# Vectors of the last layer made for one condition, and spread three and six over two feed-forwards

## The chip, the cores and the metric

The kernel runs on one core of a Trainium2 chip. The metric is the device time of one execution in microseconds (us). Before the change it is 2590.86 us, the median of three runs (2588.58 to 2592.14).

## The reference, cut to what matters

The model has two layers over 512 latent tokens and 256 context tokens of width 1024. Each layer has a feed-forward half-step, a mixer and another feed-forward half-step. Nine vectors of 1024 numbers (shift, scale and gate for each of the three parts) steer a layer; they come from a matrix product with w_mod, once for the latents' condition c and once for the context's condition c_ctx:

```python
mx = jnp.split((silu(c) @ w_mod[l] + b_mod[l])[:, None, :], 9, axis=-1)
my = jnp.split((silu(c_ctx) @ w_mod[l] + b_mod[l])[None, None, :], 9, axis=-1)
x = x + 0.5 * mx[2] * swiglu(modulate(rmsnorm(x), mx[0], mx[1]), ...)
y = y + 0.5 * my[2] * swiglu(modulate(rmsnorm(y), my[0], my[1]), ...)
ox, oy = mixer(modulate(rmsnorm(x), mx[3], mx[4]), modulate(rmsnorm(y), my[3], my[4]), ...)
x = x + mx[5] * ox
if not last: y = y + my[5] * oy
x = x + 0.5 * mx[8] * swiglu(modulate(rmsnorm(x), mx[6], mx[7]), ...)
if not last: y = y + 0.5 * my[8] * swiglu(modulate(rmsnorm(y), my[6], my[7]), ...)
```

In the last layer my[5] to my[8] are read by nothing. The output is the RMS norm of the latents.

## The kernel before, in words

Activations lie transposed, with the model's width on the partitions: eight tiles of 128 rows for each stream. Products are made in three passes from a high and a low part (`mm3`, lines 162 to 167). Weights arrive as 512 KB tiles, are cast on ScalarE (line 159) and their rest is subtracted on VectorE (line 160), three tiles ahead of their use. At most four high and four low parts are held at a time.

*The vectors.* `mod_chunks` (line 364) makes them on VectorE. One vector, numbered j from 0 to 8, has two halves of 512 columns, and each half is four chunks of 512 KB. A chunk holds two row blocks; each of them is multiplied by the condition and added into an accumulator, one per condition (`mod_add`: line 319 for the first, line 321 for the others). So a chunk is four VectorE operations of 128x512. After four chunks `mod_fold` turns and reduces each accumulator (lines 329 and 330), and after two halves `mod_sums` adds up over partitions with one small matmul on TensorE (line 337) and adds the bias on VectorE (line 346). The chunk loads (line 371, on SyncE's queue) go into two buffers, `wm`; the load of a chunk waits until the chunk two before it has been added.

*The order of the work.* All instructions are issued in one order that a planner sets. `spent` counts a planner's clock by the columns of the products, and after each group of products `poll` lets every background task whose time has come issue its next step. `spawn(..., 90.0)` starts a task 90 planner us later. In `mod_chunks` a `yield -pace` makes the next step due one pace after the last due time, and `yield 11.71` sets it 11.71 after the present clock. `drain(task)` (line 124) issues everything that is left of a task at once, other tasks that are due before it included, and moves the planner's clock up to it. Each engine then works through its own queue in the order of issue.

*The stages around the change.* The second feed-forward of layer 0 and the first of layer 1 are both `ffn_halved` (line 808), over both streams, 22 blocks of 128 columns. The first four blocks are made directly; the other 18 by `up_halved`, seven products instead of eight, whose sums are copied (line 774) and added (lines 788 to 803). At the end of each, the down products of the context and then of the latents update x and its squares, and `done` starts `norm_steps` (line 487) as a task: mean square, reciprocal root, a broadcast through TensorE (line 450), and eight tiles of the normed input (lines 511 to 517). In the last layer the mixer begins with `keys` (line 961): the four key heads for the context, then for the latents.

Before the change, layer 1's vectors 0 to 4 are made during layer 0's second feed-forward, and 5 to 8 during layer 1's first. Both tasks are drained when their feed-forward has been issued:

```python
later = self.spawn(self.mod_chunks([(l, j) for j in range(5, 9)], 9.0), 90.0)      # 1395
self.ffn_halved(l, 0, h, both, both, both, done)
self.drain(later)                                                                # 1397
```

Of the kernel before, what the change touches and what calls it, by code (L numbers as in the profile page):

```python
# [20 lines left out]
DEPTH = 2  # L21
# [8 lines left out]
CTX, LAT = 0, 1  # L30
# [51 lines left out]
class Kernel:  # L82
# [229 lines left out]
        yield  # L312
        self.mod_sums(l, j, (half,), rows[:, :32])

    def mod_add(self, acc, raw, k):
        for v in range(2):
            s = self.sc[:, k, v : v + 1]
            if k == 0:
                self.nc.vector.tensor_scalar(acc[v], raw, s, None, op0=ALU.mult)
            else:  # L320
                self.nc.vector.scalar_tensor_tensor(acc[v], raw, s, acc[v], op0=ALU.mult, op1=ALU.add)  # L321

    def mod_fold(self, acc, rows):

        nc = self.nc
        rv = rows.rearrange("p (v b) -> p v b", v=2)
        for v in range(2):
            t = self.slot("mturn")
            nc.vector.transpose(t, acc[v])
            nc.vector.tensor_reduce(rv[:, v], t.rearrange("p (b i) -> p b i", i=32), axis=mybir.AxisListType.X, op=ALU.add)  # L330
# [33 lines left out]
    def mod_chunks(self, ljs, pace):  # L364

        nc = self.nc
        steps = [(l, j, half, kk) for l, j in ljs for half in range(2) for kk in range(4)]

        def load():
            raw = self.wide("wm").rearrange("p (k n) -> p k n", k=2)  # L370
            nc.sync.dma_start(raw, self.ins["w_mod"][steps.pop(0)])
            return raw

        after = load()
        for l, j in ljs:
            rows = self.tiny(64, "mrow")
            for half in range(2):
                acc = [self.slot("macc") for _ in range(2)]
                for kk in range(4):
                    raw, after = after, load() if steps else None  # L380
                    yield -pace
                    for k in range(2):
                        self.mod_add(acc, raw[:, k], kk * 2 + k)
                self.mod_fold(acc, rows[:, half * 32 : half * 32 + 32])
            yield 11.71
            self.mod_sums(l, j, (0, 1), rows)

# [927 lines left out]
    def run(self):  # L1315
        nc = self.nc
        both = (G_CTX, G_LAT)
        halves = (G_LAT1, G_LAT2)
        self.setup()
        raws = [self.mod_load(0, 1, 0)]  # L1320
        self.load_x(CTX, self.ins["ct"])
        self.load_x(LAT, self.ins["xt"])
        raws.append(self.mod_load(0, 0, 0))
        accs, bc = {}, {}
        h = self.rows()
        for grp in both:
            for dt in range(KD):
                self.square(dt, grp, accs)
        scale = self.mod_direct(0, 1, 0, raws[0])
        for _ in range(KD + 1):  # L1330
            next(scale)
        shift = self.mod_direct(0, 0, 0, raws[1])
        ms = [self.mean_square(G_CTX, accs)]
        for _ in range(2):
            next(shift)
        ms.append(self.mean_square(G_LAT, accs))
        r = self.rsqrt(ms, NT // P, 1.0 / D, "rms")
        dg = {G_CTX: self.diag(r[:, : NTT[CTX]]), G_LAT: self.diag(r[:, NTT[CTX] :])}
        next(scale, None)
        self.scale(0, 0, LAT, 0)  # L1340
        for _ in range(KD - 1):
            next(shift)
        for grp in both:
            ps = self.rstd(grp, dg[grp])
            bc[grp] = self.slot("rstd")[:, : grp[2]]
            nc.scalar.copy(bc[grp], ps)
        next(shift, None)
        with self.tc.issue_after(self.last.ins):
            w0 = {0: self.w13()}
        raws = [self.mod_load(0, 1 - j, 1) for j in range(2)]  # L1350
        for grp in both:
            self.norm_tiles(0, 0, grp, h, range(4), bc[grp])
        self.look = LOOKAHEAD
        with self.tc.issue_after(self.last.ins):
            w0[1] = self.w13()
        scale = self.mod_halfway(0, 1, 1, raws[0])
        next(scale)
        ps = {}
        begin = ((G_CTX, 0), (G_LAT, 0), (G_LAT, 1))
        for grp, f in begin:  # L1360
            ps[grp, f] = {(f, m): self.psum("up")[:, : grp[2]] for m in range(2)}
            self.products([(ps[grp, f][f, m], w0[f][m], 0) for m in range(2)], h, grp, range(4), last=False)
        shift = self.mod_direct(0, 0, 1, raws[1])
        for _ in range(KD + 1):
            next(shift)

        def begun(g):
            next(scale, None)
            next(shift, None)
            for grp in both:  # L1370
                self.norm_tiles(0, 0, grp, h, range(4, KD), bc[grp])
            for grp, f in begin:
                self.products([(ps[grp, f][f, m], w0[f][m], 512) for m in range(2)], h, grp, range(4, KD), first=False)
                self.up({f: w0[f]}, [f], h, g, grp, ps[grp, f])
            self.up(w0, [1], h, g, G_CTX)

        self.early = True
        self.first = [self.spawn(self.mod_chunks([(0, 2)], 4.0), 10.0)]
        later = self.spawn(self.mod_chunks([(0, j) for j in range(3, 9)], 6.0), 80.0)
        for l in range(DEPTH):  # L1380
            last = l == DEPTH - 1
            grps = (G_LAT,) if last else both
            cuts = halves if last else both

            def next_norm(l, idx):
                tiles = self.rows()
                return tiles, lambda grp, accs: self.norm(l, idx, grp, accs, tiles)

            h1, done = next_norm(l, 1)
            if not last:  # L1390
                self.ffn(l, 0, h, both, both, both, done, begun)
                self.drain(later)
                self.decays()
            else:
                later = self.spawn(self.mod_chunks([(l, j) for j in range(5, 9)], 9.0), 90.0)
                self.ffn_halved(l, 0, h, both, both, both, done)
                self.drain(later)

            h2, done = next_norm(l, 2)
            self.mixer(l, h1, grps, cuts, done)  # L1400

            if not last:
                later = self.spawn(self.mod_chunks([(l + 1, j) for j in range(5)], 7.4), 90.0)
                h, done = next_norm(l + 1, 0)
            else:
                done = self.final
            (self.ffn if last else self.ffn_halved)(l, 1, h2, cuts, grps, cuts, done)
            self.drain(later)
        self.drain(*self.tasks)
# [133 lines left out]
```

## Time and profile before

| what | us |
|---|---|
| median of three runs | 2590.86 |
| the profiled execution's own time | 2592.09 |
| its span, first to last instruction | 2590.3 |
| VectorE busy | 1811.2 (70%) |
| ScalarE busy | 1015.7 (39%) |

The profile is of one execution, on the one core, with a mean granted TensorE clock of 0.99. Busy time of TensorE is modelled: matmuls overlap in its pipeline, and idle time between them is more telling than the share. A wait is put down to the instruction whose end released it.

### The profile page before, as it was taken

To read this page: it belongs to the slowest core of one execution; us is meant where nothing else is said; L and a number is where in the kernel's file an instruction comes from. 1 tells how busy PE (TensorE), PEld (TensorE's weight loads), DVE (VectorE), ACT (ScalarE), POOL (GpSimd) and SP (SyncE) were. 2 spreads that over 40 slices of the span, in tenths; PEclk is the share of its full clock that TensorE was granted. 3 is DMA by queue.
4 is the path that set the end of the run, shared out by engine and by line. 5 is a ranking of instruction groups with operands and counts; after the bars stand their busy time and mean duration, and the time that the engine had idled before them with its cause. 6 is when DMAs were issued, how large, how long until landed. Compare 5 with 4: busy or idle time off the path is not lost. (4 is left out here: it accounts for less than half of the span.)

```text
span 2590.3 us, 36708 instructions
## 1 busy us (share of the span) xinstructions
PE 2529.6 (98%) x14002; PEld 2246.6 (87%) x14002; DVE 1811.2 (70%) x3390; ACT 1015.7 (39%) x1780; POOL 276.6 (11%) x316
## 2 busy tenths in 40 slices
PE   8999999999999999999999999999999999999998
PEld 4888888888888888999899889989998888888887
DVE  6957767747977677788788858758777786633345
ACT  3211211223335444555454445545544263422223
POOL 0000000000000122422320132322310001000000
PEclk9999999999999999999999999999999999999999
DMA  7533433422222745787775457776663334232231
GB/s 273 161 108 122 139 122 114 130 74 100 85 79 60 198 106 130 180 204 180 168 196 187 110 111 195 162 179 179 145 159 122 114 97 119 91 98 98 94 102 41
DMA packets 149265, 345.37 MB, mean 133 GB/s; under 512 B 15712, under 2 KB 54112, under 8 KB 149088
## 3 DMA queue, kind: packets, MB, share of 16 engines
q1 hardware_dynamic: 101088, 276.94, 32.5%
q0 software_dynamic: 44928, 61.89, 15.0%
q10 hardware_dynamic: 3072, 4.20, 0.6%
q8 instruction: 109, 1.79, 0.3%
q14 instruction: 68, 0.56, 0.1%
HBM read 263.27 MB, written 75.50 MB: 131 GB/s over the span
## 5 line engine op out<-in xcount | busy, mean ns | idle before, releaser
L159 ACT CAST wh<-raw 128x1024 fp32r<-128x1024 f32 (+1 forms) x400 | 400.7, 1004 | 863.6 <-PE up L165 329.8
L160 DVE TENSOR_TENSOR wl<-raw,wh 128x1024 fp32r<-128x1024 f32 (+1 forms) x400 | 464.3, 1164 | 338.2 <-ACT wh L159 325.3
L164 PE MATMUL up<-h,wh 128*128 128x512 f32 (+2 forms) x1920 | 663.0, 347 | 21.9 <-ACT half L774 15.7
L165 PE MATMUL up<-h,wh 128*128 128x512 f32 (+2 forms) x1920 | 662.3, 345 | 0.2
L166 PE MATMUL up<-h,wl 128*128 128x512 f32 (+2 forms) x1920 | 661.0, 345 | 0.0
L231 POOL DMA_DIRECT2D xkept<-xpart x312 | 276.4, 1550 | 1904.2 <-ACT xpart L229 1595.0
L164 PE MATMUL down<-g,wh 128*128 128x256 f32 (+1 forms) x1264 | 425.7, 345 | 8.3 <-ACT xpart L229 4.3
L165 PE MATMUL down<-g,wh 128*128 128x256 f32 (+1 forms) x1264 | 431.2, 343 | 0.0
L166 PE MATMUL down<-g,wl 128*128 128x256 f32 (+1 forms) x1264 | 428.2, 341 | 0.4 <-DVE wl L160 0.4
L164 PEld LDWEIGHTS up<-h,wh 128*128 128x128 f32 x1920 | 365.7, 191 | 59.3 <-ACT half L774 17.9
L165 PEld LDWEIGHTS up<-h,wh 128*128 128x128 f32 x1920 | 366.6, 191 | 33.1 <-DVE h L515 0.7
L166 PEld LDWEIGHTS up<-h,wl 128*128 128x128 f32 x1920 | 366.2, 191 | 31.3
L321 DVE SCALAR_TENSOR_TENSOR macc<-wm,sc,macc 128x512 f32<-128x512 f32 x462 | 320.2, 746 | 56.5 <-DMA wm<-in_w_mod_dram 56.3
L164 PEld LDWEIGHTS down<-g,wh 128*128 128x128 f32 x1264 | 236.8, 190 | 41.0 <-ACT g L159 8.3
L165 PEld LDWEIGHTS down<-g,wh 128*128 128x128 f32 x1264 | 240.5, 190 | 28.1 <-DVE g L160 1.7
L166 PEld LDWEIGHTS down<-g,wl 128*128 128x128 f32 x1264 | 239.6, 190 | 28.3 <-DVE wl L160 0.6
L229 ACT ACTIVATE xpart<-down,gate 128x256 f32<-128x256 f32 (+1 forms) x288 | 152.5, 585 | 72.1 <-PE down L166 69.9
L663 DVE TENSOR_TENSOR silu<-silu,up 128x256 f32<-128x256 f32 (+1 forms) x84 | 48.5, 579 | 159.0 <-PE up L166 159.0
L164 PE MATMUL up<-t,wh 128*128 128x384 f32 x432 | 145.2, 336 | 0.3 <-ACT half L774 0.2
L166 PE MATMUL up<-t,wl 128*128 128x384 f32 x432 | 144.4, 334 | 0.0
L165 PE MATMUL up<-t,wh 128*128 128x384 f32 x432 | 144.4, 334 | 0.0
L700 DVE SCALAR_TENSOR_TENSOR x<-down,gate,x 128x512 f32<-128x512 f32 (+1 forms) x152 | 95.0, 634 | 65.9 <-PE down L166 65.2
(210 smaller groups left out, 3298.3 us busy)
## 6 DMA issues: line engine op xcount, KB each, us to landing
raw<-in_w_dram SPq DMA_DIRECT2D x260, 512.0 KB, 3.8
wm<-in_w_mod_dram SPq DMA_DIRECT2D x128, 512.0 KB, 4.3
xkept<-xpart POOLq DMA_DIRECT2D x160, 256.0 KB, 9.3
xkept<-xpart POOLq DMA_DIRECT2D x152, 128.0 KB, 8.6
raw<-in_w_feat_dram SPq DMA_DIRECT2D x36, 512.0 KB, 3.6
xkept<-x SPq DMA_DIRECT2D x44, 256.0 KB, 3.2
x<-xkept SPq DMA_DIRECT2D x44, 256.0 KB, 6.3
wm<-in_w_mod_dram SPq DMA_DIRECT2D x32, 256.0 KB, 5.5
```

The costliest lines, as they stand in the source:

```text
L159: self.nc.scalar.copy(hi, src)
L160: self.nc.vector.tensor_sub(lo, src, hi.bitcast(F32))
L164: nc.tensor.matmul(out, wh, xh, start=start, stop=False, skip_group_check=shared)
L165: nc.tensor.matmul(out, wh, xl, start=False, stop=False, skip_group_check=shared)
L166: nc.tensor.matmul(out, wl, xh, start=False, stop=stop, skip_group_check=shared)
L229: self.nc.scalar.activation(part, ps, AF.Copy, scale=gate)
L231: self.nc.gpsimd.dma_start(self.kept[st][:, c0 : c0 + n], part, accum_op=ALU.add)
L321: self.nc.vector.scalar_tensor_tensor(acc[v], raw, s, acc[v], op0=ALU.mult, op1=ALU.add)
L663: nc.vector.tensor_mul(t, t, ps[f, 1])
L700: nc.vector.scalar_tensor_tensor(xd, ps, self.gate(l, idx, grp[0], dt), xd, op0=ALU.mult, op1=ALU.add)
```

## The change

The last layer's vectors 5 to 8 (the mixer's gate and the second feed-forward's three) are made for the latents' condition alone: half of the adds, turns and reductions, with zeros written for the context. The context's share of other vectors stays. The vectors 0 to 2 of layer 1 are now made during layer 0's second feed-forward, at a pace of 14.0, and 3 to 8 during layer 1's first, at a pace of 7.4.

```diff
+    @staticmethod
+    def conditions(l, j):
+        return (LAT,) if l == DEPTH - 1 and j > 4 else (CTX, LAT)
+
-    def mod_add(self, acc, raw, k):
-        for v in range(2):
+    def mod_add(self, acc, raw, k, vs=(CTX, LAT)):
+        for v in vs:
...
-    def mod_fold(self, acc, rows):
+    def mod_fold(self, acc, rows, vs=(CTX, LAT)):
         nc = self.nc
         rv = rows.rearrange("p (v b) -> p v b", v=2)
         for v in range(2):
+            if v not in vs:
+                nc.vector.memset(rv[:, v], 0.0)
+                continue
             t = self.slot("mturn")
...
             for half in range(2):
-                acc = [self.slot("macc") for _ in range(2)]
+                vs = self.conditions(l, j)
+                acc = {v: self.slot("macc") for v in vs}
                 for kk in range(4):
                     raw, after = after, load() if steps else None
                     yield -pace
                     for k in range(2):
-                        self.mod_add(acc, raw[:, k], kk * 2 + k)
-                self.mod_fold(acc, rows[:, half * 32 : half * 32 + 32])
+                        self.mod_add(acc, raw[:, k], kk * 2 + k, vs)
+                self.mod_fold(acc, rows[:, half * 32 : half * 32 + 32], vs)
...
-                later = self.spawn(self.mod_chunks([(l, j) for j in range(5, 9)], 9.0), 90.0)
+                later = self.spawn(self.mod_chunks([(l, j) for j in range(3, 9)], 7.4), 90.0)
...
-                later = self.spawn(self.mod_chunks([(l + 1, j) for j in range(5)], 7.4), 90.0)
+                later = self.spawn(self.mod_chunks([(l + 1, j) for j in range(3)], 14.0), 90.0)
```

## Rows read from the trace of the kernel before

**Rows 1.** The page, busy time, share and instructions of each engine.
```profile
PE 2529.6 (98%) x14002; PEld 2246.6 (87%) x14002; DVE 1811.2 (70%) x3390; ACT 1015.7 (39%) x1780; POOL 276.6 (11%) x316
```

**Rows 2.** Busy time by stretch (start:end, length, PE, PEld, DVE, ACT, POOL, clock, DMA).
```profile
894.30:1433.20 538.90, 525.24 (x2980) 488.75 (x2979) 423.39 (x731) 269.68 (x473) 127.12 (x144) 0.99 0.68 168
1433.20:1979.10 545.90, 530.21 (x2978) 494.51 (x2977) 398.38 (x685) 269.53 (x472) 128.16 (x144) 0.98 0.64 155
```

**Rows 3.** What TensorE waited for, first stage, then second (total, times, longest).
```profile
PE up L164 <- ACT half L774: 4.3, 2, 4.2
PE down L164 <- ACT g L159: 3.9, 2, 2.0
...
PE up L164 <- ACT half L774: 11.6, 5, 3.1
```

**Rows 4.** Timeline around 1253 us: TensorE, then VectorE (start, length, operation).
```profile
1250.98 0.33 PE L164 MATMUL up<-t,wh 128*128 128x384 f32 x1
1251.15 0.33 PE L165 MATMUL up<-t,wh 128*128 128x384 f32 x1
...
1253.50 0.75 DVE L321 SCALAR_TENSOR_TENSOR macc<-wm,sc,macc 128x512 f32<-128x512 f32 x1 [5.91 <-DMA wm<-in_w_mod_dram]
1254.29 0.56 DVE L788 TENSOR_TENSOR half<-up,half 128x384 f32<-128x384 f32 x1
```

**Rows 5.** VectorE's groups of the vectors, first stage, then second (busy, mean ns, idle before).
```profile
L321 DVE SCALAR_TENSOR_TENSOR macc<-wm,sc,macc 128x512 f32<-128x512 f32 x140 | 97.5, 747 | 20.4 <-DMA wm<-in_w_mod_dram 20.4
...
L321 DVE SCALAR_TENSOR_TENSOR macc<-wm,sc,macc 128x512 f32<-128x512 f32 x112 | 77.0, 745 | 31.2 <-DMA wm<-in_w_mod_dram 31.2
...
L329 DVE STREAM_TRANSPOSE mturn<-macc 128x512 f32<-128x512 f32 x16 | 10.7, 695 | 0.0
L330 DVE TENSOR_REDUCE mrow<-mturn 128x16 f32<-128x512 f32 x16 | 10.3, 666 | 0.0
```

**Rows 6.** Busy time by stretch, behind two of the stalls: the granted clock is 0.50.
```profile
1256.40:1259.80 3.40, 3.40 (x13) 3.40 (x12) 3.34 (x6) 1.56 (x2) 0.00 (x0) 0.50 0.28 94
...
1898.10:1901.50 3.40, 3.40 (x12) 3.40 (x12) 3.37 (x7) 2.47 (x4) 0.00 (x0) 0.50 0.46 157
```

**Rows 7.** The fold matmuls, first stage, then second (ns, first and last start).
```profile
L337 PE MATMUL mods<-mrow,cs x10: 217/246/275, 1080.5 to 1394.8; 128*128 128x64 f32 x10
...
L337 PE MATMUL mods<-mrow,cs x8: 217/246/275, 1633.4 to 1923.6; 128*128 128x64 f32 x8
```

**Rows 8.** Timeline of TensorE where the last layer's mixer begins.
```profile
1979.15 0.28 PE L164 MATMUL kq<-h,wh 128*128 128x256 f32 x1
...
1983.68 1.06 PE L434 MATMUL ms<-ones,acc 128*128 128x128 f32 x8
1984.50 0.36 PE L165 MATMUL kq<-h,wh 128*128 128x256 f32 x1
...
1988.77 1.02 PE L450 MATMUL rstd<-diag,ones 128*128 128x512 f32 x2
1989.23 0.68 PE L164 MATMUL kq<-h,wh 128*128 128x256 f32 x1
```

**Rows 9.** Timeline of VectorE there.
```profile
1980.62 1.22 DVE L160 TENSOR_TENSOR wl<-raw,wh 128x1024 fp32r<-128x1024 f32 x1
1981.75 1.48 DVE L426 TENSOR_TENSOR acc<-acc,sq 128x512 f32<-128x512 f32 x2
1984.78 0.16 DVE L176 TENSOR_SCALAR rms<-ms 128x4 f32<-128x4 f32 x1 [1.54 <-PE ms L434]
...
1986.95 0.87 DVE L441 TENSOR_SCALAR diag<-cs,rms 128x128 f32<-128x128 f32 x4
1989.83 2.07 DVE L511 SCALAR_TENSOR_TENSOR ht<-x,G,rstd 128x512 f32<-128x512 f32 x3 [2.01 <-PE rstd L450]
...
2000.08 0.75 DVE L517 SCALAR_TENSOR_TENSOR h<-ht,mod,h 128x512 fp32r<-128x512 f32 x1 [0.26 <-ACT h L513]
```

**Rows 10.** Loads of the chunks by line 371, whole span: issue to landing.
```profile
DMA to landing us min/median/max: 3.3/4.3/10.9
```

## The prediction

> **What bounds the kernel now.** I read the page's busy line first, then the stages, then what TensorE waits for in the two stages that the change touches. TensorE is the bound: it is busy for 2529.6 of 2590.3 us [rows 1]. The chain on the page has only a few instructions, so it doesn't help; the stages do. I cut them at TensorE's own transitions. The second feed-forward of layer 0 runs from 894.3 to 1433.2 us (538.9 us), the first of layer 1 from 1433.2 to 1979.1 us (545.9 us), and the last layer's mixer begins at 1979.15 us with its first kq product, directly behind the last down product [rows 2, 8]. Both feed-forwards issue the same products, so a different length means different stalls.
>
> The waits that a modulation chunk can cause are in [rows 3]. In the first stage they are 4.3 us behind the copies of line 774 (nearly all one wait of 4.2) and 3.9 us behind line 159. In the second they are 11.6 us in five waits. One in the first stage looks like this: VectorE sat 5.91 us in front of a line-321 add whose weights hadn't landed, and line 788 of the feed-forward stood queued behind it [rows 4]. VectorE waits like that for 20.4 us in the first stage and 31.2 us in the second [rows 5]. After such a stall the granted clock is 0.50, the 1.2 GHz level, for 3.4 us; I found one such stretch in the first stage and four in the second behind these waits [rows 6] (the first and the last of the five). Thirteen matmuls fill 3.4 us there; at the 0.17 us between neighbours of [rows 4] they would take 2.2, so each costs 1.2 us. Sums: 8.2 + 1.2 = 9.4 us and 11.6 + 4 x 1.2 = 16.4 us. Without them both stages would take 529.5 us (538.9 - 9.4 and 545.9 - 16.4), so these are all that separates them.
>
> **The change part by part.**
>
> *The planner's account.* The chunks are placed by a clock that counts 0.000422 us per column of each product. One halved feed-forward is, from the code, 4 blocks x 16 x 3 x 768 columns (62.2), 18 blocks x 28 x 3 x 384 (245.0) and 22 x 8 x 3 x 768 for down (171.1): 478.3 planner us, plus 0.43 per finished vector. A vector costs 8 paces + 11.71. Before, the five of the first stage need 90 + 5 x 70.9 = 444.6, and the four of the second 90 + 4 x 83.7 = 424.8: both end in time. The trace agrees: the last sums run at 1394.8 and 1923.6 us, 38 and 55 us ahead of the stages' ends [rows 7], and the real stages are 1.12 and 1.14 times the planner's.
>
> After the change the first stage needs 90 + 3 x (8 x 14 + 11.71) = 461.1, and still fits into 479.6. The second needs 90 + 6 x (8 x 7.4 + 11.71) = 515.5, but has 480.5. At its end about four chunks of the last vector (the whole second half) are not yet issued. drain(later) on line 1397 then issues them at once, before a single product of the mixer. That is the step that decides.
>
> *What drain issues, in order.* The latents' norm task stands among the tasks: mean square, rsqrt, diagonals; one chunk; the broadcast and the eight norm tiles; then three chunks, the fold, and the fold matmul of mod_sums on TensorE's in-order queue. Behind that matmul stand all kq products. Before, the context's kq products covered the norm; now nothing does. The clock of events:
> - The last x, squares and adds end at 1983.23 us before, with a 1.22 us weight split between them that now comes later [rows 9]: 1982.1. The fourth chunk of the last vector and its half fold (two adds, a transpose, a reduce) fall about here: between nothing and 2.5 us; I take 2.0, so the mean square starts at 1984.2.
> - From mean square to first norm tile it was 1983.68 to 1989.83 [rows 8, 9], 0.95 of it TensorE reaching the broadcast late. The chunk behind the diagonals adds 0.3: 1989.7.
> - Norm tiles: 1989.83 to 2000.83 = 11.0 us [rows 9]: 2000.7.
> - The next chunk's two adds, 1.4 us (0.745 each [rows 5], overlapping a little): 2002.1. Only now is its buffer of the two free, and SyncE can issue the last chunk's load. Landing took 3.3 us at the least, 4.3 in the median and 10.9 at the most [rows 10]; I take the median, since the stores of x were issued some 15 us earlier, and 0.2 for the issue: 2006.6.
> - Last chunk: two adds, transpose, reduce, 2.6 us [rows 5]: 2009.2; fold matmul 0.3 [rows 7]: 2009.5 against 1979.15, so 30.4 us. The mean square's and broadcast's matmuls (0.82 and 0.46 us by the starts in [rows 8]) were in the old stream: 29.1.
> - The fourth kq weight's split (1.2 us) is now queued behind the eight adds of line 346 (up to 1.6 us); kq reaches that weight after nine matmuls of 0.12: 2.0 us more. Nothing to 3 us.
> - Clock: one stretch at half, 1.2 us; bounds 0 and 3.6.
>
> Cost: 32.3 us. Lowest: no half fold, a 3.3 us load, no split, no clock: 26. Highest: a 10.9 us load and three stretches: 41.
> The Trainium skill (DMA: Bandwidth & Descriptors, Anatomy of one DMA) fits a transfer as 2.0 us plus its bytes at 436 GB/s, for 512 KB an estimate of 3.2 us; the trace's least is 3.3 and its median 4.3, and by the page's figure the cost would be 31.2 us.
>
> *What it removes.* Four vectors of the last layer lose the context's half: 8 x (8 adds + transpose + reduce) = 64 x 0.745 + 8 x 1.35 = about 58 us of VectorE, less eight memsets of 16 columns, which I put at 0.15 us each by the small operations in [rows 9] (bounds 0 and 0.5 each). VectorE is not the bound, so this pays only through stalls. All 8 of the saved shares are gone from the first stage (20 halves by condition become 12; the second keeps 16). No load is saved: the stages' chunks go from 40 and 32 to 24 and 48.
>
> *What that is worth.* First stage, pace 14: 3.1 chunks in one cycle of two blocks (42.8 planner us) instead of 5.8; VectorE seldom runs into a load that has not landed. Of 9.4 us I leave 3 (0 to 9.4). Second stage, pace 7.4: 44 chunks in time. At the first stage's old rate, which is the same pace, 9.4 x 44/40 = 10.3; at its own old rate, 16.4 x 44/32 = 22.6. I take the one with the same pace: 10.3 of 16.4, for a lone-condition chunk is no slower. Gain 6.4 + 6.1 = 12.5 us, between 25.8 (all stalls go) and -6.2.
>
> Sum: +32.3 - 12.5 = +19.8 us on the profiled execution's 2592.1, which lies 1.2 over the median: 2610.7 on the scale of the median; I say 2610.
>
> **The rivals.**
> 1. *The chunks end in time* (8%). The poll points or the drains inside the stage would have to carry the planner's clock on by 35 us. Against it: old ends at 1394.8 and 1923.6 fit the count. Then the gain alone remains: 2590.9 - 12.5 = 2578, faster. It decides below 65 planner us a vector.
> 2. *The stalls go altogether, the drain is cheap* (8%): 26 - 25.8, no change, 2591. For it: with 24 slower chunks in the first stage all loads may be in time there. Against: the pace in the second stage becomes denser. The Trainium skill (Trainium Kernel Development and Optimization, Best Practices) asks for two buffers so that loads lie beside compute; here two buffers leave the 20.4 and 31.2 us of waits of [rows 5].
> 3. *The denser second stage stalls more* (14%): its own old rate, 22.6, and a drain near 38: +38 - 6.4 + 6.2 = +38, 2629. For it: 31.2 us of waits for loads there at a slower pace.
> 4. *The change does not do what it says*: the context's gate and half-step vectors of the last layer would have to be read somewhere; the mixer and feed-forward run there on the latents alone, so I give it nothing.
>
> **How the numbers follow.** The forecast has 70%: 2610, in its own bounds 2598 to 2624. The range 2595 to 2630 takes in rival 3 and leaves out rival 1 and half of rival 2. A difference under 0.2% (5.2 us) can't be told from none here. Slower: the forecast, rival 3 and a little of rival 2, 0.86; within: 0.06; faster: 0.08.
>
> **What would show it.** A gap of 25 to 35 us in TensorE between the last down product of layer 1's first feed-forward and the first kq product, ended by the fold's reduce, with the last 512 KB chunk load issued inside it; sums in the first stage at three places, in the second at five and then one in the gap; waits behind line 774 fewer in the first stage. If the last sums stand ahead of the last down product, the forecast is wrong; if the gap is there but under 20 us, a load or norm was sized wrongly.

## The result and the profile after

The changed kernel takes 2606.04 us (median of four runs, 2604.84 to 2609.0) against 2590.96 (median of four): a ratio of 1.0068, 95% interval 1.0054 to 1.0082. It is slower by 15 us; 2610 had been forecast, in a range of 2595 to 2630. Its profiled execution took 2604.84 us, with a span of 2603.0.

The first view is the page: busy time of each engine, then two of the lines that cut the span into 40 slices (busy tenths of TensorE, and its granted clock).

```profile
PE 2520.9 (97%) x14002; PEld 2239.3 (86%) x14002; DVE 1762.0 (68%) x3318; ACT 1015.5 (39%) x1780; POOL 276.1 (11%) x316
...
PE   8999999999999999999999999999995999999998
...
PEclk9999999999999999999999999999997999999999
```

TensorE lost no instruction, and VectorE lost 49 us of work [rows 1]. In the 31st slice TensorE's busy share falls to 5 tenths and its mean clock to 7. That slice holds the border between layer 1's first feed-forward and its mixer. The next view is busy time by stretch: the two feed-forwards, the gap between them and the mixer, the mixer.

```profile
893.20:1422.80 529.60, 521.06 (x2975) 486.99 (x2974) 370.18 (x631) 269.89 (x472) 127.49 (x144) 1.00 0.65 155
1422.80:1960.00 537.20, 524.55 (x2980) 488.67 (x2978) 392.05 (x685) 268.69 (x471) 127.32 (x144) 0.99 0.68 170
1960.00:1992.90 32.90, 4.82 (x14) 2.75 (x13) 26.81 (x55) 8.38 (x12) 0.00 (x0) 0.57 0.35 116
1992.90:2221.40 228.50, 224.06 (x1237) 193.84 (x1237) 154.37 (x373) 91.55 (x187) 7.02 (x8) 0.99 0.34 96
```

Against [rows 2] the first feed-forward is 9.3 us shorter (538.9 to 529.6), the second 8.7 us (545.9 to 537.2), and 32.9 us are new, in which TensorE works for 4.8. The mixer took 229.4 us before and 228.5 now. Everything else moved the span by about 1 us. So the change gained 18 us and paid 32 for it.

TensorE's timeline shows the gap; where rows of before answer, they are [rows 8].

```profile
1959.81 0.39 PE L166 MATMUL down<-g,wl 128*128 128x512 f32 x1
1966.54 2.08 PE L443 MATMUL ms<-ones,acc 128*128 128x128 f32 x8 [6.35 <-DVE acc L435]
1971.76 2.08 PE L459 MATMUL rstd<-diag,ones 128*128 128x512 f32 x2 [3.14 <-DVE diag L450]
1992.43 0.69 PE L345 MATMUL mods<-mrow,cs 128*128 128x64 f32 x2 [18.60 <-DVE mrow L338]
1992.88 0.56 PE L164 MATMUL kq<-h,wh 128*128 128x256 f32 x1
1993.24 0.41 PE L165 MATMUL kq<-h,wh 128*128 128x256 f32 x1
```

Before, kq followed the last down product at once and the norm's two small groups of matmuls slipped in between. Now they stand alone, then comes a wait of 18.60 us for the fold's reduction (mrow), and only then kq. VectorE's timeline shows what it did meanwhile; [rows 9] answer to it.

```profile
1962.22 0.70 DVE L337 STREAM_TRANSPOSE mturn<-macc 128x512 f32<-128x512 f32 x1
1962.85 0.65 DVE L435 TENSOR_TENSOR acc<-acc,sq 128x512 f32<-128x512 f32 x1
1963.42 0.68 DVE L338 TENSOR_REDUCE mrow<-mturn 128x16 f32<-128x512 f32 x1
1964.01 0.74 DVE L863 SCALAR_TENSOR_TENSOR x<-down,gate,x 128x512 f32<-128x512 f32 x1
1964.67 1.21 DVE L160 TENSOR_TENSOR wl<-raw,wh 128x1024 fp32r<-128x1024 f32 x1
1965.80 0.69 DVE L435 TENSOR_TENSOR acc<-acc,sq 128x512 f32<-128x512 f32 x1
...
1973.87 2.06 DVE L520 SCALAR_TENSOR_TENSOR ht<-x,G,rstd 128x512 f32<-128x512 f32 x3 [0.99 <-PE rstd L459]
...
1984.45 0.74 DVE L526 SCALAR_TENSOR_TENSOR h<-ht,mod,h 128x512 fp32r<-128x512 f32 x1
1985.11 2.32 DVE L326 SCALAR_TENSOR_TENSOR macc<-wm,sc,macc 128x512 f32<-128x512 f32 x3
...
1989.37 1.54 DVE L326 SCALAR_TENSOR_TENSOR macc<-wm,sc,macc 128x512 f32<-128x512 f32 x2 [1.78 <-DMA wm<-in_w_mod_dram]
1990.94 0.71 DVE L337 STREAM_TRANSPOSE mturn<-macc 128x512 f32<-128x512 f32 x1
...
1991.69 0.69 DVE L338 TENSOR_REDUCE mrow<-mturn 128x16 f32<-128x512 f32 x1
```

The first half's fold (1962.22 and 1963.42) lies in front of the last x, the norm tiles run from 1973.87 to 1985.2, then three adds, a wait of 1.78 us for the last load, two adds and the second half's fold.

The stalls inside the feed-forwards, first stage, then second (TensorE's waits: total, times, longest; then VectorE's for the loads, second stage). [rows 3] and [rows 5] answer.

```profile
PE up L164 <- ACT half L783: 2.2, 2, 1.9
...
PE up L164 <- ACT half L783: 5.0, 3, 4.2
PE down L164 <- ACT g L159: 2.3, 2, 2.0
...
DVE macc L326 <- DMA wm<-in_w_mod_dram: 22.4, 11, 9.2
```

Line 774 of before is line 783 here. Its waits fell from 4.3 to 2.2 us and from 11.6 to 5.0; those behind line 159 went from the first stage to the second. The long ones (2.0 us) are waits behind a fold: its two transposes and two reductions, here from 1563.83 to 1566.2 us, stand in front of the add whose cast the down products need at 1567.24 us, and before the change it looks the same at 1034.90 us.

### The profile page after: what moved, and what is told of

Same layout as the page of the kernel before. It is cut to its first block, busy times and chain, and to the rows that moved or that the text cites. A ratio compares the mean times of both kernels' runs of the same rounds, so it can differ in the third digit from the quotient of the medians.

```text
span 2603.0 us, 36628 instructions
## 1 busy us (share of the span) xinstructions
PE 2520.9 (97%) x14002; PEld 2239.3 (86%) x14002; DVE 1762.0 (68%) x3318; ACT 1015.5 (39%) x1780; POOL 276.1 (11%) x316
## 5 line engine op out<-in xcount | busy, mean ns | idle before, releaser
L326 DVE SCALAR_TENSOR_TENSOR macc<-wm,sc,macc 128x512 f32<-128x512 f32 x406 | 284.9, 745 | 36.4 <-DMA wm<-in_w_mod_dram 35.5
```

## The experiments

Each run's ratio is to runs of the kernel before on the same chip. The two theories: the drained fold matmul in front of kq costs the 32 us (mine); or the second stage's denser work and VectorE's lateness there cost it, drain or not.

**The drain behind the key products.** The same chunks are left over, but are issued after kq.

```diff
-                self.drain(later)
-            self.mixer(l, h1, grps, cuts, done)
+            self.mixer(l, h1, grps, cuts, done, (lambda: self.drain(later)) if last else None)
...
             keys()
+            behind()
             tap_task = convolution()
```

> The changed kernel, with its drain moved from in front of the last layer's mixer to behind the issue of its key products. Same vectors, same paces, same chunks left over. Theory (the fold matmul of the last vector stands on TensorE's in-order queue in front of all key products, and that costs the 32 us between the feed-forward and the mixer): the first key product follows the last down product at once, the norm and the left-over chunks run beside the key products, and the time is 2606 - 32 = 2574 us (2569 to 2581). Rival (VectorE itself is late there: it has the chunks, the fold and the norm tiles to do in any order, so the latents' key products wait as long): 2595 us or more, with a wait for the normed input in front of the latents' key products.

Measured: 2574.56 us, ratio 0.9945 (0.9932 to 0.9957). Moving the drain alone turns the slower kernel into one faster than before. TensorE at the border, then the stretches, the same three of stage, stage and mixer:

```profile
1960.10 0.39 PE L166 MATMUL down<-g,wl 128*128 128x512 f32 x1
1960.32 0.28 PE L164 MATMUL kq<-h,wh 128*128 128x256 f32 x1
...
893.60:1423.30 529.70, 521.10 (x2976) 487.12 (x2975) 370.30 (x631) 269.86 (x473) 127.09 (x144) 1.00 0.65 156
1423.30:1960.30 537.00, 524.54 (x2979) 488.88 (x2978) 391.91 (x685) 268.73 (x472) 127.19 (x144) 0.99 0.68 170
1960.30:2190.70 230.40, 226.22 (x1248) 195.34 (x1247) 181.07 (x428) 99.68 (x199) 7.02 (x8) 0.99 0.39 112
```

The feed-forwards are those of the changed kernel to 0.2 us, and the mixer begins at their end. In the mixer's first 40 us TensorE waited 0.3 us for the diagonals and 0.3 for the normed input: VectorE did the chunks, the fold and the tiles in time, so the rival falls. The mixer's one longer wait, 3.4 us for squares at 2178 us, stands near its other end, and the kernel before has it too (3.3 us).

**An earlier start.** The six vectors begin 45 planner us into the stage, and all end before the drain.

```diff
-... for j in range(3, 9)], 7.4), 90.0)
+... for j in range(3, 9)], 7.4), 45.0)
```

> The changed kernel, with the start of the six vectors 45 instead of 90 planner us after the second stage's beginning. They then need 45 + 425.5 = 470.5 of 480.5 planner us and nothing is left for the drain. Theory: the gap of 32 us goes, some stalls come where chunks now lie beside the direct blocks and the differences, 2574 + 3 = 2577 us (2571 to 2585). Rival (the dense pace of the second stage, not the drain, is what costs): as the changed kernel or slower, 2606 us.

Measured: 2581.07 us, ratio 0.9969 (0.9958 to 0.998). Again no gap; the second stage takes 542.4 us in this profile, 5 more than in the changed kernel, with 10.1 us of waits behind line 783 in two places. The profiled execution took 2584.93 us, 3.9 over the median. Its first stage, whose instructions are the same, took 534.2 us here and 529.6 there, so a stage's length in one profile is good to some 5 us.

**Only the sums left to the drain.** The start at 66:

```diff
-... for j in range(3, 9)], 7.4), 90.0)
+... for j in range(3, 9)], 7.4), 66.0)
```

> The changed kernel, drain where it was, with the six vectors started 66 instead of 90 planner us after the second stage's beginning: 66 + 425.5 = 491.5 of 480.5, so that all chunks are added in time and only the last vector's sums are left to the drain. Theory (the gap is as long as what VectorE must still do before the fold matmul): no chunk and no fold stands in the gap, but the mean square, the diagonals and the broadcast do, about 12 us from last down to first key product instead of 33: 2574.6 + 12 = 2587 us (2581 to 2593). Rival (any drained step there costs the whole norm of the latents, 25 us or more): 2600 us or more.

Measured: 2580.98 us, ratio 0.9967 (0.9954 to 0.998), 6 us under the expectation and just under its range. TensorE's timeline at the border, then VectorE's chunk work there:

```profile
1962.75 2.07 PE L443 MATMUL ms<-ones,acc 128*128 128x128 f32 x8 [3.95 <-DVE acc L435]
1967.96 2.08 PE L459 MATMUL rstd<-diag,ones 128*128 128x512 f32 x2 [3.14 <-DVE diag L450]
1969.83 0.53 PE L345 MATMUL mods<-mrow,cs 128*128 128x64 f32 x2
1970.11 0.56 PE L164 MATMUL kq<-h,wh 128*128 128x256 f32 x1
...
1960.15 0.74 DVE L326 SCALAR_TENSOR_TENSOR macc<-wm,sc,macc 128x512 f32<-128x512 f32 x1
...
1961.42 0.70 DVE L337 STREAM_TRANSPOSE mturn<-macc 128x512 f32<-128x512 f32 x1
...
1962.62 0.67 DVE L338 TENSOR_REDUCE mrow<-mturn 128x16 f32<-128x512 f32 x1
```

The gap is 11.5 us (1958.6 to 1970.1), near the 12 expected; the fold matmul no longer waits, and the rival falls. I had expected a gap free of chunk work, but one add of the last chunk and the last fold still stand in it. The two adds of that chunk follow each other in `mod_chunks`, yet VectorE did them at 1942.70 and 1960.15 us, so its queue isn't throughout in the order of the planner's steps. The gap is thus as long as what VectorE still owes in front of the fold matmul: 11.5 us with the norm's round trip, an add and a fold, 32.9 with the norm tiles, four more chunks and a second fold.

About 4 of the 6 us show as a mixer of 227.4 instead of 230.4 us and a second stage of 536.0 instead of 537.0. The norm's two groups of matmuls (1.3 us by the starts in [rows 8]), the two waits of 0.3 us and the fold matmul stood in the first experiment's mixer and stand in the gap here, so I had counted them twice. The rest is not traced.

**One condition alone, with the old split.**

```diff
+    def conditions(l, j):
+        return (LAT,) if l == DEPTH - 1 and j > 4 else (CTX, LAT)
...
 (five vectors at 7.4, then four at 9.0, as before)
```

> Only the first part of the change: the last layer's vectors 5 to 8 for one condition, with the old split (five vectors at pace 7.4, four at 9.0). Theory (stalls come of VectorE's queue held up by the chunks, fewer adds shorten them): first stage as before at 538.9 us, second stage 545.9 - 8 = 538 us, no gap, 2591 - 8 = 2583 us (2578 to 2589). Rival (the stalls are waits for the loads of chunks, and as many are loaded): 2591 us, within 3.

Measured: 2587.75 us, ratio 0.9994 (0.9985 to 1.0002): not told apart from before, which took 2588.91 us on this chip. Both expectations were reckoned from 2591: as a time, 2587.75 lies inside my theory's range and 0.25 us outside the rival's. As a ratio my 2583 would be 0.997, outside the interval, and the rival's 1.000 is inside, so the rival was right. VectorE's waits in the second stage, before and then in this run, show where the saved time went (the loads' were 31.2 us before, [rows 5]):

```profile
DVE wl L160 <- ACT wh L159: 84.7, 39, 8.4
...
DVE wl L160 <- ACT wh L159: 108.7, 40, 8.5
DVE macc L326 <- DMA wm<-in_w_mod_dram: 48.2, 12, 9.0
```

Of the 46.9 us of busy time saved on VectorE there (398.4 to 351.5 us), 17.0 came back as waiting for the same loads and 24.0 as waiting for ScalarE's casts. TensorE still waited 9.5 us in five places behind line 783 (11.6 before). The profiled execution took 2593.17 us, 5.4 over the median, so these are no exact sizes.

**The split alone, both conditions.**

```diff
-... for j in range(5, 9)], 9.0)    -... for j in range(5)], 7.4)
+... for j in range(3, 9)], 7.4)    +... for j in range(3)], 14.0)
```

> Only the second part of the change: vectors 0 to 2 at pace 14.0, then 3 to 8 at pace 7.4, all for both conditions. Theory: the gap grows by the context's adds, turns and reductions in the chain, from 33 to about 38 us, and the second stage has more stalls with twice the adds in four of its vectors, 537 to 545 us: 2606 + 5 + 8 = 2619 us (2611 to 2629). Rival (the second condition's work is hidden on an engine that is not the bound): 2606 us, within 4.

Measured: 2621.57 us, ratio 1.0123 (1.0109 to 1.0137). The stages take 530.9 and 546.1 us and the gap 36.5; the fold matmul's wait grows to 22.17 us:

```profile
2008.28 0.69 PE L337 MATMUL mods<-mrow,cs 128*128 128x64 f32 x2 [22.17 <-DVE mrow L330]
```

So the first stage's gain comes of the split (three vectors at pace 14.0 instead of five at 7.4; number and pace are not told apart), and in the dense second stage one condition is worth 9 us in the stage and 4 in the gap.

**The split for both conditions, with the drain behind kq.** The kernel of the first experiment, with `conditions` always `(CTX, LAT)`.

> All vectors for both conditions, with the new split and paces, and the drain behind the key products. It tells what the one condition is worth when no gap is there. Theory (fewer adds in VectorE's queue shorten stalls): the second stage at 541 instead of 537 us, 2574.6 + 5 = 2580 us (2576 to 2588). Rival (the second condition's work is hidden in both stages): 2575 us, within 3.

Measured: 2585.86 us, ratio 0.9981 (0.9972 to 0.999), stages 530.6 and 546.4 us. One condition is worth 11.3 us here (2585.86 to 2574.56, from two sets of runs; by the ratios 0.36%, 9.3 us), more than the 5 expected. Of the 9.4 us by which the second stage is longer, the norm of the context near its end shows most. TensorE waited 4.7 us for the diagonals there, where the first experiment has no such wait, and 3.4 for the squares instead of 1.5. Between the first and the last step of that reciprocal root VectorE did nine adds of the chunks here (9.2 us in all) and two in the first experiment (4.9 us).

```profile
PE rstd L459 <- DVE diag L450: 4.7, 1, 4.7
PE down L164 <- ACT g L159: 3.9, 2, 2.0
PE up L164 <- ACT half L783: 3.8, 2, 3.3
PE ms L443 <- DVE acc L435: 3.4, 1, 3.4
```

**The kernel before, chunks loaded once.**

```diff
-        after = load()
+        held = [load() for _ in range(2)] if once else None
...
-                    raw, after = after, load() if steps else None
+                    raw = held[kk % 2]
```

> The kernel before, with the chunks of layer 1's vectors loaded only twice and those two tiles used for all chunks (so layer 1's vectors come out of the wrong weights); every add, turn, reduction and sum stays. Theory (the stalls behind line 774 are waits of VectorE's queue for loads of chunks; those behind line 159 are folds): the waits for loads go and with them 4.3 + 11.6 us and five stretches at half clock of 1.2 us, 2589 - 20 = 2569 us (2564 to 2576). Rival (they come of the adds themselves, which hold up VectorE's queue): 2589 us, within 5.

Measured: 2564.5 us, ratio 0.99 (0.9885 to 0.9915). The two stages:

```profile
893.40:1426.40 533.00, 523.63 (x2980) 487.32 (x2979) 422.87 (x731) 269.48 (x473) 127.89 (x144) 1.00 0.59 133
1426.40:1951.00 524.60, 520.59 (x2977) 486.99 (x2976) 398.33 (x685) 269.66 (x472) 128.15 (x144) 1.00 0.58 131
```

With every add still there, all waits behind line 774's kind are gone, VectorE waits for no chunk, and no clock falls behind them; the 3.9 us behind folds stay in the first stage. So the stalls behind line 774 came of the loads, and the stages are 5.9 and 21.3 us shorter without them. In the second that is 5 more than I had read off, about what two profiles differ by. The run takes away the loads' wait together with their traffic, and doesn't tell these two apart.

**Four and five, the drain behind kq.**

```diff
-... for j in range(3, 9)], 7.4)    -... for j in range(3)], 14.0)
+... for j in range(4, 9)], 8.2)    +... for j in range(4)], 10.5)
```

> One condition for the last layer's vectors 5 to 8, vectors 0 to 3 at pace 10.5 in the first stage and 4 to 8 at pace 8.2 in the second, the drain behind the key products. Theory (stalls grow with the chunks that fall into one cycle of two blocks): 4.1 and 5.2 chunks in a cycle instead of 3.1 and 5.8, first stage 531, second 534 us, 2574.6 - 2 = 2573 us (2568 to 2579). Rival (which chunk meets which transfer decides, and not how many there are): anywhere between 2570 and 2590, with single waits of 3 to 5 us at other places.

Measured: 2564.44 us, ratio 0.9898 (0.9882 to 0.9915): 1% faster than before, and faster than the changed kernel by 42 us. That is below my theory's range and the rival's, so the size of the gain was foreseen by neither. The stages take 527.6 and 531.7 us in a profiled execution of 2569.47 us, 5.0 over the median:

```profile
895.80:1423.40 527.60, 521.87 (x2977) 487.07 (x2976) 394.95 (x672) 269.01 (x472) 127.38 (x144) 1.00 0.67 164
1423.40:1955.10 531.70, 523.80 (x2977) 488.83 (x2976) 377.70 (x661) 271.19 (x473) 127.33 (x144) 0.99 0.66 166
...
PE up L164 <- ACT half L783: 0.5, 1, 0.5
```

The waits behind line 783 are down to 0.5 us in each stage. That the count of chunks in a cycle alone sets the stalls is not shown: the first stage has more chunks here than with three vectors and is 2 us shorter, within what two profiles differ by.

## Why the prediction was right

*The planner's account* held. Sums run at three places in the first stage and five in the second, and the sixth in the gap. The first experiment shows by itself that the drain is the step that decides.

*The cost* was forecast as 32.3 us and is 32.0 (a gap of 32.9, the mixer 0.9 shorter), but several terms were off and made up for each other, so that the sum came this close is in part luck:
- The mean square began 6.5 us after the last down product's end at 1960.03, not 5.05. The weight split that I had moved behind the drain (1.1 us) stayed in front of the last add: VectorE did it at 1964.67.
- From the mean square to the first norm tile it took 7.3 us, not 5.5: both small groups of matmuls ran at half clock, 2.08 us each instead of 1.06 and 1.02 [rows 8].
- The tiles took 11.3 us, with one add among them (11.0 forecast). From there to the fold matmul it was 7.2 us, not 8.5: one of the next chunk's adds stood among the tiles and the other right behind them, so SyncE issued the last load at 1985.88, and it landed in 3.5 us, not in the median's 4.3 [rows 10]. The Trainium skill's fit (DMA: Bandwidth & Descriptors, Anatomy of one DMA), an estimate of 3.2 us for 512 KB, is given there for transfers that GpSimd issues. This one, issued by SyncE, came within 0.3 us of it; three smaller loads were issued behind it, and its 512 KB made up about 150 of the 204 GB/s that were moved in these 3.5 us.
  SyncE's timeline, and the landing of that load:

```profile
1985.88 0.33 SPq L379 DMA_DIRECT2D wm<-in_w_mod_dram  x1
...
DMA to landing us min/median/max: 3.5/3.5/3.5
```

- The 2.0 us for the fourth kq weight did not occur, since its split was done early. The half clock took about 1.1 us from kq, near the 1.2 forecast: twelve matmuls at 0.21 instead of 0.12.

*The gain* was the term mis-sized: 12.5 us forecast, 18.0 measured. In the first stage I left 3 us of stalls, and it took 529.6 us against the 529.5 that I had reckoned without any. This gain is beyond the spread of profiles: three vectors at pace 14.0 took 529.5 to 534.2 us in six of them, five at 7.4 took 538.9 and 542.1. But 529.5 is not the least a stage takes, nor are the waits that I listed all that separates the two stages: with no load to wait for they took 533.0 and 524.6 us.

In the second stage I took the old first stage's rate, 10.3 us, and 7.7 were left. Here two errors made up for each other. With both conditions the stage took 546.1 us, 16.6 over 529.5 and as long as before the change; the lone condition, to which I had given nothing, was worth 8.9 of them. That it saves nothing at the old split and pace shows that it isn't the saved work of VectorE as such. Why it pays where chunks follow each other closely is shown only for the context's norm, and the rest is open. (The 58 us that I had summed up for VectorE are 49 on the page; the forecast doesn't use them.)

*The rivals.* The chunks did not end in time, and the drain was not cheap. The denser second stage, which rival 3 had stall more, stalled less, though only with the lone condition.

## What to carry to other kernels

Background work that is paced by a clock has to fit into its stage: add up paces, waits and start before changing the split. What is left over is issued at the drain, and where the drain stands in front of an in-order engine's next stage, one small matmul holds up everything behind it. Move the drain behind the first work that doesn't need its result; here that alone was worth 32 us, and with it a balanced split made the kernel 1% faster than before.

## What the runs showed of the hardware

The granted clock was 1.00 in the first 4.9 us of the gap. It stayed at its half level, 1.2 GHz, from there to the gap's end, although two groups of matmuls ran in it, and for the first 2.7 us of kq. Busy time by stretch, from 1964.9 us to the first kq product:

```profile
1964.90:1992.90 28.00, 4.62 (x13) 2.75 (x13) 21.91 (x47) 6.23 (x9) 0.00 (x0) 0.50 0.28 89
```

I had priced the clock for the products behind the gap only; it also lengthened the norm's round trip inside it. And a zero written over 16 columns took 0.07 us on VectorE, half of what I had put for it.
